# A mixer and expert layer: gates of three dense blocks added into cleared DRAM matrices instead of built by one-hot products

## The chip, the cores and the metric

The kernel runs on one core of a Trainium2 chip. Its time is the device time of one execution in microseconds. Five engines work side by side: TensorE (PE, matmuls into PSUM), VectorE (DVE), ScalarE (ACT), GpSimd (POOL) and SyncE (SP). Each executes its own list of instructions strictly in order and waits on semaphores. Transfers are issued on SP's queue, or, where an index list gives the addresses, on POOL's (indirect DMAs).

## What is computed

A layer of 1024 tokens with 1024 channels: a matrix-memory recurrence and a windowed attention side by side, merged by gates, and then an expert network (PEER). For each token, each of 8 heads picks 16 of 16384 experts by two lists of 128 sub-keys; an expert is one row of `expert_down` and one of `expert_up`.

```python
top_s, top_i = lax.top_k(s, K)                       # per head, two lists of 128 scores, K = 16
cand_s = (top_s[:, :, 0, :, None] + top_s[:, :, 1, None, :]).reshape(t, PEER_HEADS, K * K)
cand_i = (top_i[:, :, 0, :, None] * N_KEYS + top_i[:, :, 1, None, :]).reshape(t, PEER_HEADS, K * K)
best_s, best_pos = lax.top_k(cand_s, K)
idx = jnp.take_along_axis(cand_i, best_pos, axis=-1)
gate = jax.nn.softmax(best_s, axis=-1)
u = expert_down[idx]
act = jax.nn.gelu(jnp.einsum('td,thkd->thk', xb, u), approximate=False)
vv = expert_up[idx]
return jnp.einsum('thk,thkd->td', gate * act, vv)
```

## The kernel before

The tokens form 8 blocks of 128. Four groups of two blocks (0 and 1, 2 and 3, 4 and 5, 6 and 7) run one after the other through `front`: projections, attention, recurrence, gates, residual, and the expert scores. `front` streams its weights in 82 parts of 512 KB per group (`wpart`, L209, four buffers). ScalarE rounds a part to a high half and VectorE makes the low half (L215), and TensorE multiplies both (L231 to L233); some products run in plain fp32 (L229). At the end of `front` VectorE adds the residual (L614), a norm follows (L166 to L169), and TensorE computes the queries of the experts and the scores (L640). The first weight part of the next group then needs VectorE again (L215).

`topk` runs on VectorE for the blocks of the group before, at low priority, and gives each token 128 picks: row, column and gate. Then there are two ways.

- Blocks 0, 6 and 7 are sparse. `down` fetches the picked expert rows from DRAM, 128 gathers per block, each of 128 rows of 4 KB (one per token; L743, an indirect DMA on POOL), and VectorE takes the dot product of each (L756); `up` adds the weighted rows (L770). The gathers of block 0's `down` run beside the groups 1 to 3, into two buffers of a pool `gather`. Its dots are tied by order alone (no semaphore) to matmuls of the groups, the anchors: from 0.40 to 0.95 of their list (`PACE0`, `PACE1`). The gathers of `up` for block 0 and all others run in the dense stage.
- Blocks 1 to 5 are dense. All 16384 experts are computed for their 640 tokens, one column of 128 experts at a time, and multiplied by a gate matrix that is zero but for the picks. `spread` builds this matrix. For each token VectorE makes two one-hot matrices of the 128 picks (rows weighted by the gate, L727; columns, L730; a quarter of the latter on ScalarE, L732 and L733), and a 128 x 128 matmul contracts them (L735). ScalarE copies four tokens at a time into a chunk of 16 (`stage`, L736, two buffers), and SP writes the chunk to `gate_d` in DRAM (L738), 1 MB in pieces of 256 bytes. A call of four tokens comes between the matmuls of the next group's `front` (`fill`, 0.75 of one per place): block 1 in group 1, blocks 2 and 3 in group 2, blocks 4 and 5 in group 3.

The dense stage (`dense`) loads the gates of four columns at a time (L841) and multiplies them into the activations of 640 tokens (L816). In the built order a scheduler places each instruction by priority and by its own estimate of when its inputs are there; each engine then keeps that order.

Of the kernel before, what the change touches and what calls it, by code (L numbers as in the profile page):

```python
# [11 lines left out]
F32 = mybir.dt.float32  # L12
F32R = mybir.dt.float32r
I32 = mybir.dt.int32
# [5 lines left out]
NOSYNC = mybir.DependencyInfo(mybir.DependencyClass.NoSync, mybir.DependencyReason.DATA)  # L20

# [14 lines left out]
DENSE = (1, 2, 3, 4, 5)  # L36
ND = P * len(DENSE)
# [5 lines left out]
PACE0, PACE1 = 0.4, 0.95  # L43
# [11 lines left out]
def layout(inputs):  # L55
# [29 lines left out]
    a["iota"] = np.arange(P, dtype=np.float32)[None]  # L85
    return {k: np.ascontiguousarray(v) for k, v in a.items()}


def build(nc, tc, a, out, dbg=None):
# [8 lines left out]
    gp = pool("gather", 2)  # L98
# [34 lines left out]
    pos = const("pos", [P, NB], dt=I32, pool=st)  # L133
    freq = bcast("freq", 8, st)
# [59 lines left out]
    gate_d = dp.tile([P, P // GJ, ND // GT, GJ, GT], F32, name="gate_d")  # L194
# [452 lines left out]
    def topk(b):  # L647
# [15 lines left out]
        for qh in range(4):  # L663
# [23 lines left out]
            for p, n in ((0, 17), (1, 16)):  # L687
# [7 lines left out]
                else ks.tile([P, 8, 16], F32, name="dgate", bufs=2))  # L695
# [12 lines left out]
        if b in DENSE:  # L708
            r["spread"] = spread(ef, gate, DENSE.index(b))
        return r  # L710

    def spread(ef, gate, k):
# [5 lines left out]
        for c in range(P // GT):  # L718
            stage = ks.tile([P, P, GT], F32, name="stage", bufs=2)
# [20 lines left out]

    def fetch(p, table, idx, s):
        t = p.tile([P, D], F32, name="g")
        G.indirect_dma_start(out=t, out_offset=None, in_=a[table],  # L743
                             in_offset=bass.IndirectOffsetOnAxis(ap=idx[:, s:s + 1], axis=0))
        return t

    def down(r, b, pace, p):
# [14 lines left out]
        r["coef"] = coef  # L762

# [10 lines left out]
    def dense():  # L774
# [26 lines left out]
        def hidden(j, g):  # L801
# [13 lines left out]
            av_ = act.rearrange("p (c t) -> p c t", t=GT)  # L815
            V.tensor_tensor(av_, av_, g, ALU.mult)  # L816
# [22 lines left out]
        for n in range(P // EG):  # L839
            g = tp.tile([P, ND // GT, GJ, GT], F32, name="g")  # L840
            SY.dma_start(g, gate_d[:, n])  # L841
            new = []
            for e in range(EG):
                new.append(hidden(EG * n + e, g[:, :, e, :]))
# [37 lines left out]
    names = names[int(PACE0 * len(names)):int(PACE1 * len(names))]  # L882
    pace = iter([names[i * len(names) // P] for i in range(P)])
    down(res[0], 0, pace, gp)
# [22 lines left out]
```

## Time and profile before

| | us |
|---|---|
| three runs, median | 3551.62 |
| lowest, highest | 3545.43, 3563.59 |
| the profiled execution | 3545.12 |
| its span in the profile | 3543.4 |
| TensorE busy in the span | 3378.6 (95%) |
| VectorE | 2743.1 (77%) |
| ScalarE | 1363.0 (38%) |
| POOL | 985.7 (28%) |

Busy is the time in which an engine works on an instruction; transfers that it issues are not in it. The granted clock of TensorE is 0.966 of full speed over the span. The four groups end at about 370, 782, 1221 and 1714 us, told by their score matmuls (L640), and the dense stage runs from about 1746 to 3520. A row of busy times by stage shows how full an engine is, a row of waits says what an engine stood still for, and the chain that ended last names which work set the time at each moment.

### The profile page before, as it was taken

To read this page: it belongs to the slowest core of one execution; us is meant where nothing else is said; L and a number is where in the kernel's file an instruction comes from. 1 tells how busy PE (TensorE), PEld (TensorE's weight loads), DVE (VectorE), ACT (ScalarE), POOL (GpSimd) and SP (SyncE) were. 2 spreads that over 40 slices of the span, in tenths; PEclk is the share of its full clock that TensorE was granted. 3 is DMA by queue.
4 is the path that set the end of the run, shared out by engine and by line. 5 is a ranking of instruction groups with operands and counts; after the bars stand their busy time and mean duration, and the time that the engine had idled before them with its cause. 6 is when DMAs were issued, how large, how long until landed. Compare 5 with 4: busy or idle time off the path is not lost.

```text
span 3543.4 us, 55473 instructions
## 1 busy us (share of the span) xinstructions
PE 3378.6 (95%) x20579; PEld 3044.3 (86%) x20579; DVE 2743.1 (77%) x6406; ACT 1363.0 (38%) x2730; POOL 985.7 (28%) x772
## 2 busy tenths in 40 slices
PE   7999999999998789989799999999999999999999
PEld 7898988888887678887688898999989999898998
DVE  5332689739898468988598988888888888889985
ACT  6652567338574346635322222222222222222221
POOL 0000000110001221110004654545455455545542
PEclk9999999999999888999899999999999999999999
DMA  4344434874378874686727988889888888888884
GB/s 149 108 143 166 164 115 145 256 261 141 117 212 252 274 247 150 206 244 174 252 101 276 329 307 321 321 284 329 285 315 305 294 321 299 312 308 302 325 288 160
DMA packets 386670, 846.66 MB, mean 239 GB/s; under 512 B 189280, under 2 KB 195168, under 8 KB 382304
## 3 DMA queue, kind: packets, MB, share of 16 engines
q1 hardware_dynamic: 275808, 440.42, 37.7%
q0 software_dynamic: 110592, 402.70, 32.5%
q8 instruction: 162, 2.65, 0.3%
q14 instruction: 108, 0.88, 0.1%
HBM read 780.11 MB, written 62.91 MB: 238 GB/s over the span
## 4 chain that ended last, share of the span: by engine, by line
PE 66%; DVE 13%; issue 8%; DMA 7%; POOL 3%; ACT 3%; SPq 0%; POOLq 0%; DVEq 0%; ACTq 0%
PE ph L809 19%; PE pj L229 8%; PE po L830 6%; PE po L833 6%; PE po L834 6%; PE pj L231 4%; PE pj L233 4%; PE pj L232 4%; DMA g<-down,idx 3%; POOL g L743 3%; DVE oi L727 2%; PE at L735 2%; DMA w<-wmain 1%; DVE g L756 1%; DMA g<-up,idx 1%
## 5 line engine op out<-in xcount | busy, mean ns | idle before, releaser
L743 POOL DMA_INDIRECT g<-down,idx x384 | 480.2, 1250 | 1769.3 <-DVE act L756 879.2
L743 POOL DMA_INDIRECT g<-up,idx x384 | 505.3, 1316 | 732.8 <-DVE acc L770 373.9
L756 DVE CUSTOM_DVE_ANT_0 g<-g,xb 128x1024 f32<-128x1024 f32 x384 | 462.6, 1219 | 167.2 <-DMA g<-down,idx 166.6
L770 DVE SCALAR_TENSOR_TENSOR acc<-g,coef,acc 128x1024 f32<-128x1024 f32 x384 | 491.7, 1281 | 46.8 <-DMA g<-up,idx 36.8
L830 PE MATMUL po<-hu,ah 128*128 128x512 f32 x1280 | 499.2, 390 | 2.3 <-DVE y L836 2.3
L809 PE MATMUL ph<-xbh,hd 128*128 128x320 f32 x2048 | 470.6, 311 | 31.7 <-ACT hd L797 22.8
L833 PE MATMUL po<-lu,ah 128*128 128x512 f32 x1280 | 498.5, 389 | 0.0
L834 PE MATMUL po<-hu,al 128*128 128x512 f32 x1280 | 498.1, 389 | 0.0
L809 PE MATMUL ph<-xbh,ld 128*128 128x320 f32 x2048 | 470.5, 311 | 5.3 <-DVE ld L798 5.3
L809 PE MATMUL ph<-xbl,hd 128*128 128x320 f32 x2048 | 469.9, 311 | 0.0
L797 ACT CAST hu<-rawu 128x1024 fp32r<-128x1024 f32 x128 | 131.5, 1051 | 738.9 <-PE po L834 557.0
L809 PEld LDWEIGHTS ph<-xbh,hd 128*128 128x128 f32 x2048 | 346.6, 189 | 35.3 <-ACT hd L797 23.2
L215 DVE TENSOR_TENSOR wlo<-w,whi 128x1024 fp32r<-128x1024 f32 x200 | 243.3, 1218 | 142.1 <-ACT whi L214 142.0
L809 PEld LDWEIGHTS ph<-xbh,ld 128*128 128x128 f32 x2048 | 345.1, 189 | 7.0 <-DVE ld L798 6.7
L809 PEld LDWEIGHTS ph<-xbl,hd 128*128 128x128 f32 x2048 | 345.6, 189 | 0.0
L214 ACT CAST whi<-w 128x1024 fp32r<-128x1024 f32 x200 | 209.3, 1047 | 235.9 <-DMA w<-wmain 100.1
L836 DVE TENSOR_TENSOR y<-po,y 128x512 f32<-128x512 f32 x320 | 218.2, 685 | 89.0 <-PE po L834 88.5
L830 PEld LDWEIGHTS po<-hu,ah 128*128 128x128 f32 x1280 | 240.3, 188 | 53.9 <-DVE y L836 4.7
L834 PEld LDWEIGHTS po<-hu,al 128*128 128x128 f32 x1280 | 240.3, 188 | 50.5 <-DVE al L820 0.3
L833 PEld LDWEIGHTS po<-lu,ah 128*128 128x128 f32 x1280 | 240.3, 188 | 48.5
L232 PE MATMUL pj<-wlo,hT 128*128 128x256 f32 x832 | 244.9, 295 | 23.9 <-DVE wlo L215 23.9
L231 PE MATMUL pj<-whi,hT 128*128 128x256 f32 x832 | 245.9, 296 | 1.1 <-ACT whi L214 1.1
(266 smaller groups left out, 6670.2 us busy)
## 6 DMA issues: line engine op xcount, KB each, us to landing
w<-wmain SPq DMA_DIRECT2D x328, 512.0 KB
rawd<-downT SPq DMA_DIRECT2D x128, 512.0 KB
rawu<-up SPq DMA_DIRECT2D x128, 512.0 KB
gate_d<-stage SPq DMA_DIRECT2D x40, 1024.0 KB
g<-gate_d SPq DMA_DIRECT2D x32, 1280.0 KB
x<-x SPq DMA_DIRECT2D x16, 512.0 KB
sc_d<-sc SPq DMA_DIRECT2D x16, 512.0 KB
sc<-sc_d SPq DMA_DIRECT2D x32, 256.0 KB
```

The costliest lines, as they stand in the source:

```text
L215: V.tensor_tensor(lo, t, hi.bitcast(F32), ALU.subtract)
L229: ins = T.matmul(ps, lh(c), rh(c), start=first, stop=last)
L231: T.matmul(ps, lh(c), rh(c), start=first, stop=False)
L232: T.matmul(ps, lh(c), rl(c), start=False, stop=False)
L743: G.indirect_dma_start(out=t, out_offset=None, in_=a[table], in_offset=bass.IndirectOffsetOnAxis(ap=idx[:, s:s + 1], axis=0))
L756: ins = V.tensor_tensor_reduce(out=t, in0=t, in1=xb, scale=1.0, scalar=0.0, op0=ALU.mult, op1=ALU.add, accum_out=act[:, s:s + 1])
L770: ins = V.scalar_tensor_tensor(acc, t, g, acc, ALU.mult, ALU.add)
L809: ins = T.matmul(ps[:, u, 0:W], w[:, c, :], x[:, c, u * W:u * W + W], start=first, stop=last)
L830: first = T.matmul(o, ah[:, tok], uh[:, cols], start=(e == 0), stop=False)
L833: T.matmul(o, ah[:, tok], ul[:, cols], start=False, stop=False)
L834: ins = T.matmul(o, al[:, tok], uh[:, cols], start=False, stop=(e == EG - 1))
L836: V.tensor_tensor(y[:, k, cols], o, y[:, k, cols], ALU.add)
```

## The change

The gate matrices of blocks 1 to 3 no longer come from one-hot products. Three DRAM matrices `cells`, of 8 MB each, are cleared by 192 DMAs of 128 KB from a zeroed tile. `topk` computes for each pick the place in the block's matrix (`cell`), and `scatter` adds the gates there: 128 indirect DMAs per block on POOL, each of 128 values of 4 bytes (one per token) with an addition at the target. A token has no pick twice within a head, but can in two heads. So the first addition of a head waits until the 16 of the head before have landed (`SYNC`), and the other 15 follow it in order alone. The additions are tied by order to the gathers of block 0 (`BESIDE`: which gathers, for which block). `down` of block 0 starts earlier (0.32), the gather pool has three buffers, and `stage` has one. Blocks 4 and 5 keep the one-hot products. The dense stage loads the gates in two tiles and multiplies in two instructions, of 384 and 256 tokens.

```diff
-PACE0, PACE1 = 0.4, 0.95
+PACE0, PACE1 = 0.32, 0.95
+ADDED = (1, 2, 3)
+SPREAD = (4, 5)
+BESIDE = {1: (2, 44), 2: (58, 92), 3: (92, 126)}
+ZP = 64
...
-    gp = pool("gather", 2)
+    gp = pool("gather", 3)
...
+    cells = {b: dp.tile([P // EG, P, EG, P], F32, name=f"cells{b}") for b in ADDED}
+    flat = {b: t.rearrange("n i e t -> (n i e t)") for b, t in cells.items()}
+    none = st.tile([P, P * P // ZP], F32, name="none")
+    V.memset(none, 0.0)
+    clear = iter([flat[b].rearrange("(z p f) -> z p f", z=ZP, p=P)[z] for b in ADDED for z in range(ZP)])
...
     def wpart(i, q, split):
         t = wp.tile([P, 4, 256], F32, name="w", bufs=WB)
         SY.dma_start(t, a["wmain"][i, :, 4 * q:4 * q + 4, :])
+        for z in [next(clear, None)]:
+            if z is not None:
+                SY.dma_start(z, none)
...
+        if b in ADDED:
+            r["cell"] = cell = ks.tile([P, P], I32, name="cell", bufs=NA)
...
+            V.tensor_scalar(cell, pf[:, 0], float(P), tokc, ALU.mult, ALU.add)
+        if b in SPREAD:
+            r["spread"] = spread(ef, gate, SPREAD.index(b))
...
-            stage = ks.tile([P, P, GT], F32, name="stage", bufs=2)
+            stage = ks.tile([P, P, GT], F32, name="stage", bufs=1)
...
+    def scatter(b, pace):
+
+        cell, vals = res[b]["cell"], res[b]["gate"].rearrange("p h k -> p (h k)")
+        views = bass_types.dram_disjoint_views(flat[b][:, None], 16)
+        done = []
+        for h in range(8):
+            new = []
+            for s in range(16):
+                c = 16 * h + s
+                ins = G.indirect_dma_start(out=views[s], out_offset=bass.IndirectOffsetOnAxis(ap=cell[:, c:c + 1], axis=0),
+                                           in_=vals[:, c:c + 1], in_offset=None, compute_op=ALU.add)
+                if s == 0:
+                    for d in done:
+                        tc.add_manual_dep(ins.ins, d, SYNC, reason="heads")
+                else:
+                    after(ins, new[0])
+                after(ins, next(pace, None))
+                new.append(ins.ins.name)
+            done = new
...
-            V.tensor_tensor(av_, av_, g, ALU.mult)
+            V.tensor_tensor(a1_, a1_, g[0], ALU.mult)
+            V.tensor_tensor(a2_, a2_, g[1], ALU.mult)
...
+            ga = tp.tile([P, NA, EG, P], F32, name="ga")
+            gs = tp.tile([P, len(SPREAD) * P // GT, GJ, GT], F32, name="g")
+            for k, b in enumerate(ADDED):
+                SY.dma_start(ga[:, k], cells[b][n])
+            SY.dma_start(gs, gate_d[:, n])
...
+    down(res[0], 0, paced(PACE0, PACE1), gp)
+    for b, (lo, hi) in BESIDE.items():
+        scatter(b, iter([fetched[lo + i * (hi - lo) // P] for i in range(P)]))
```

The lines move: the gather is L773 in the changed kernel, the additions L804, the dots L787, the residual L631, the norm L175 to L178 and the weight split L232. In the rows below `cells_155` and `cells_156` are the matrices of blocks 1 and 2, and a count at a row's end says how often it repeats.

POOL's whole order before, apart from its set-up: block 0's gathers of `down`, then everything else.

```order
L898 MEMSET const-uint8-127 128x1
L903 UNCONDITIONAL_BRANCH
L743 DMA g<-down,idx 128x1024 x128
L743 DMA g<-up,idx 128x1024 x128
L743 DMA g<-down,idx 128x1024 x256
```

POOL now, in the last third of group 1, where block 1's additions stand between the gathers 26 to 31 (counted from 0).

```order
L804 DMA cells_155<-dgate,cell 2097152x1 x6
L773 DMA g<-down,idx 128x1024
L804 DMA cells_155<-dgate,cell 2097152x1 x10
L773 DMA g<-down,idx 128x1024
L804 DMA cells_155<-dgate,cell 2097152x1 x6
L773 DMA g<-down,idx 128x1024
L804 DMA cells_155<-dgate,cell 2097152x1 x10
L773 DMA g<-down,idx 128x1024
L804 DMA cells_155<-dgate,cell 2097152x1 x8
```

Here 40 of block 1's 128 additions moved in between gathers that stood side by side before.

POOL now, at the end of group 2, with block 2's additions between the gathers 79 to 87.

```order
L804 DMA cells_156<-dgate,cell 2097152x1 x11
L773 DMA g<-down,idx 128x1024
L804 DMA cells_156<-dgate,cell 2097152x1 x8
L773 DMA g<-down,idx 128x1024
L804 DMA cells_156<-dgate,cell 2097152x1 x6
L773 DMA g<-down,idx 128x1024
L804 DMA cells_156<-dgate,cell 2097152x1 x7
L773 DMA g<-down,idx 128x1024
L804 DMA cells_156<-dgate,cell 2097152x1 x11
L773 DMA g<-down,idx 128x1024
L804 DMA cells_156<-dgate,cell 2097152x1 x5
L773 DMA g<-down,idx 128x1024
```

The row after these is 23 additions, then one gather, and so on to the end of block 2's 128. VectorE's order at the same place before, at the residual and the norm of group 2:

```order
L614 TENSOR_TENSOR x<-pj,x 128x512
L730 TENSOR_SCALAR oj<-iota,cols 128x128
L727 TENSOR_SCALAR oi<-iota,cols 128x128
L730 TENSOR_SCALAR oj<-iota,cols 128x128
L727 TENSOR_SCALAR oi<-iota,cols 128x128
L730 TENSOR_SCALAR oj<-iota,cols 128x128
L727 TENSOR_SCALAR oi<-iota,cols 128x128 x2
L730 TENSOR_SCALAR oj<-iota,cols 128x128
L727 TENSOR_SCALAR oi<-iota,cols 128x128 x4
L756 ISA g,act<-g,xb 128x1024
L756 ISA act 128x1
```

And now (an `ISA` row with `g,act` is a dot product, the row behind it reads its sum):

```order
L631 TENSOR_TENSOR x<-pj,x 128x512
L787 ISA g,act<-g,xb 128x1024
L787 ISA act 128x1
L787 ISA g,act<-g,xb 128x1024
L787 ISA act 128x1
L631 TENSOR_TENSOR x<-pj,x 128x512 x2
L175 TENSOR_TENSOR rs_t<-rs_y 128x2
L176 SCALAR_TENSOR_TENSOR rs_t<-ms,rs_t 128x2
L177 TENSOR_SCALAR rs_t<-rs_t 128x2
L178 TENSOR_TENSOR rs<-rs_t,rs_y 128x2
L787 ISA g,act<-g,xb 128x1024
```

The one-hot compares between the residual sums are gone, and five dots (gathers 83 to 87) now stand between the norm and the first four weight splits (L232) of group 3; before, 15 dots stood there.

## Rows read from the trace of the kernel before

**Rows 1.** Busy time by stage; columns in the first row, counts in brackets.
```profile
core 0: us, PE busy (x) PEld busy (x) DVE busy (x) ACT busy (x) POOL busy (x), PEclk, DMA share, GB/s
0.00:370.00 370.00, 339.55 (x2262) 303.28 (x2262) 138.67 (x377) 184.63 (x420) 0.20 (x4) 0.96 0.42 141
370.00:782.00 412.00, 396.14 (x2681) 353.61 (x2682) 298.65 (x1093) 223.80 (x534) 28.27 (x26) 0.95 0.58 185
782.00:1221.00 439.00, 410.27 (x2726) 364.91 (x2726) 365.44 (x1352) 248.80 (x610) 46.24 (x45) 0.94 0.66 202
1221.00:1714.00 493.00, 446.78 (x2929) 392.80 (x2928) 379.36 (x1358) 252.50 (x608) 67.88 (x57) 0.92 0.67 204
1746.00:3520.00 1774.00, 1757.68 (x9863) 1605.55 (x9862) 1525.50 (x2096) 442.27 (x542) 843.09 (x640) 1.00 0.82 291
```

**Rows 2.** The same for the one-hot products (L735) alone, groups 1 and 2.
```profile
370.00:782.00 412.00, 39.76 (x256) 35.38 (x256) 0.95 0.58 185
782.00:1221.00 439.00, 79.38 (x512) 72.71 (x512) 0.94 0.66 202
```

**Rows 3.** Waits of VectorE and POOL while block 0's gathers run: total, times, longest.
```profile
DVE g L756 <- DMA g<-down,idx: 125.1, 49, 5.8
...
POOL g L743 <- DVE act L756: 610.9, 81, 144.8
```

**Rows 4.** POOL in order of time, dense stage: start, length, instruction, idle before it.
```profile
1883.14 0.94 POOL L743 DMA_INDIRECT g<-up,idx  x1 [0.30 <-issue]
1884.39 0.94 POOL L743 DMA_INDIRECT g<-up,idx  x1 [0.30 <-issue]
```

**Rows 5.** POOL in order of time, start of group 3.
```profile
1240.18 1.68 POOL L743 DMA_INDIRECT g<-down,idx  x1 [3.70 <-DVE act L756]
1242.46 1.68 POOL L743 DMA_INDIRECT g<-down,idx  x1 [0.60 <-DVE act L756]
```

**Rows 6.** The chain that ended last, block 1's products: start, length, pieces.
```profile
602.46 2.15 PE at L735 x16
```

**Rows 7.** Busy time in seven stretches of groups 1 to 3, columns as in Rows 1.
```profile
661.00:730.00 69.00, 67.47 (x368) 61.13 (x369) 34.94 (x69) 11.60 (x26) 15.57 (x15) 1.00 0.81 273
730.00:771.00 41.00, 34.84 (x164) 29.75 (x164) 9.26 (x18) 13.38 (x33) 6.38 (x6) 0.92 0.71 235
1139.00:1177.00 38.00, 32.96 (x178) 29.13 (x176) 28.00 (x87) 11.11 (x29) 8.74 (x9) 0.96 0.89 271
1177.00:1239.00 62.00, 44.45 (x215) 38.13 (x213) 26.44 (x64) 21.31 (x50) 16.06 (x16) 0.80 0.87 271
1239.00:1280.00 41.00, 28.70 (x198) 27.75 (x199) 22.18 (x32) 11.11 (x15) 12.91 (x9) 0.80 0.78 290
1367.00:1483.00 116.00, 112.52 (x716) 94.59 (x714) 98.45 (x360) 60.15 (x145) 18.78 (x16) 0.88 0.54 181
1556.00:1600.00 44.00, 40.07 (x220) 35.91 (x221) 37.54 (x126) 8.57 (x17) 8.47 (x8) 0.93 0.77 248
```

**Rows 8.** The one-hot products alone in two of these stretches.
```profile
1139.00:1177.00 38.00, 11.56 (x76) 11.04 (x76) 0.96 0.89 271
1177.00:1239.00 62.00, 6.97 (x30) 5.87 (x28) 0.80 0.87 271
```

**Rows 9.** DMA during one chunk's write: GB/s in 40 slices, and its queue.
```profile
GB/s 0 0 0 0 0 0 0 0 0 53 233 219 217 222 215 218 217 218 218 217 218 218 218 219 217 218 217 217 215 222 218 217 212 217 217 221 211 104 0 0
q1 hardware_dynamic: 4112, 1.05, 72.1%
```

**Rows 10.** Groups of instructions: line, engine, operation, count, busy us, mean ns, idle.
```profile
L735 PE MATMUL at<-oj,oi 128*128 128x128 f32 x1280 | 201.6, 290 | 23.1 <-DVE oj L730 13.1 <-DVE oi L727 5.0 <-ACT oj L733 4.8
L816 DVE TENSOR_TENSOR act<-act,g 128x640 f32<-128x640 f32 x128 | 104.7, 818 | 6.0 <-ACT act L814 6.0
L215 DVE TENSOR_TENSOR wlo<-w,whi 128x1024 fp32r<-128x1024 f32 x200 | 243.3, 1218 | 142.1 <-ACT whi L214 142.0
```

More of the change, by code (lines that the diff above doesn't have):

```diff
@@ L8 @@
 import concourse.tile as tile
+from concourse import bass_types
 from concourse import mybir
@@ L36 @@
 DENSE = (1, 2, 3, 4, 5)
+ADDED = (1, 2, 3)
+SPREAD = (4, 5)
+NA = len(ADDED)
+BESIDE = {1: (2, 44), 2: (58, 92), 3: (92, 126)}
+ZP = 64
 ND = P * len(DENSE)
@@ L133, in build @@
     pos = const("pos", [P, NB], dt=I32, pool=st)
+    tokc = const("tokc", [P, 1], pool=st)
     freq = bcast("freq", 8, st)
@@ L707, in topk @@
             probe("gate", gate, b)
-        if b in DENSE:
-            r["spread"] = spread(ef, gate, DENSE.index(b))
+        if b in ADDED:
+            r["cell"] = cell = ks.tile([P, P], I32, name="cell", bufs=NA)
+            part = kp.tile([P, 2, P], I32, name="part", tag="eq", bufs=1)
+            pf = kp.tile([P, 2, P], F32, name="partf", tag="sc")
+            V.tensor_copy(part[:, 0], ef[:, 1])
+            V.tensor_single_scalar(part[:, 1], part[:, 0], EG - 1, ALU.bitwise_and)
+            V.tensor_single_scalar(part[:, 0], part[:, 0], 2, ALU.logical_shift_right)
+            V.tensor_copy(pf, part)
+            V.scalar_tensor_tensor(pf[:, 0], pf[:, 0], float(P), ef[:, 0], ALU.mult, ALU.add)
+            V.scalar_tensor_tensor(pf[:, 0], pf[:, 0], float(EG), pf[:, 1], ALU.mult, ALU.add)
+            V.tensor_scalar(cell, pf[:, 0], float(P), tokc, ALU.mult, ALU.add)
+        if b in SPREAD:
+            r["spread"] = spread(ef, gate, SPREAD.index(b))
         return r
@@ L739, in spread @@
                 yield
+    fetched = []
     def fetch(p, table, idx, s):
         t = p.tile([P, D], F32, name="g")
-        G.indirect_dma_start(out=t, out_offset=None, in_=a[table],
-                             in_offset=bass.IndirectOffsetOnAxis(ap=idx[:, s:s + 1], axis=0))
+        ins = G.indirect_dma_start(out=t, out_offset=None, in_=a[table],
+                                   in_offset=bass.IndirectOffsetOnAxis(ap=idx[:, s:s + 1], axis=0))
+        fetched.append(ins.ins.name)
         return t
@@ L839, in dense @@
         for n in range(P // EG):
-            g = tp.tile([P, ND // GT, GJ, GT], F32, name="g")
-            SY.dma_start(g, gate_d[:, n])
+            ga = tp.tile([P, NA, EG, P], F32, name="ga")
[3 more added lines that the diff above has]
+            SY.dma_start(gs, gate_d[:, n])
             new = []
             for e in range(EG):
-                new.append(hidden(EG * n + e, g[:, :, e, :]))
+                new.append(hidden(EG * n + e, (ga[:, :, e, :], gs[:, :, e, :])))
                 if n == 0 and e == 0:
@@ L881, in build, with paced @@
     names = anchors["front"]
-    names = names[int(PACE0 * len(names)):int(PACE1 * len(names))]
-    pace = iter([names[i * len(names) // P] for i in range(P)])
-    down(res[0], 0, pace, gp)
+    def paced(lo, hi):
+        return iter([names[int((lo + i * (hi - lo) / P) * len(names))] for i in range(P)])
+    down(res[0], 0, paced(PACE0, PACE1), gp)
+    for b, (lo, hi) in BESIDE.items():
+        scatter(b, iter([fetched[lo + i * (hi - lo) // P] for i in range(P)]))
     inner.close()
```

9 lines of the change are left out of this document (6 added, 3 removed).

## The prediction

> **What bounds the kernel now.** I read the busy time by stage first [rows 1]. Four groups of two blocks run one after the other to 1714 us, and a dense stage follows. TensorE is busy 340 of 370 us in group 0, 396 of 412 in group 1, 410 of 439 in group 2, 447 of 493 in group 3, and 1758 of 1774 in the dense stage. So TensorE's instruction stream sets the end, and what can be won in the groups is the one-hot products on it and its gaps. The one-hot products (L735) have 40 us of TensorE's busy time in group 1 and 79 in group 2 [rows 2]. The gaps come mostly from the gathers of block 0. VectorE waits 125 us for gathered rows while these run, and GpSimd (POOL) waits 611 us for VectorE to free one of two buffers [rows 3]. VectorE works in order, so a late gather holds the weight splits that TensorE needs next.
>
> POOL is nearly idle: 142 us busy in 128 gathers over groups 1 to 3 [rows 1]. It is the engine that the change loads. Its prices: two gathers without a wait between them start 1.25 us apart (0.94 busy, 0.30 between) [rows 4]; at worst, beside VectorE's dots, 2.28 us (1.68 and 0.60) [rows 5]; on average 142.4/128 + 0.30 = 1.41 us.
>
> **The change part by part.**
>
> *The one-hot products of blocks 1 to 3 go.* That is 768 of 1280 matmul records [rows 10], with their VectorE, ScalarE and write work. Back to back, 16 records take 2.15 us on the chain [rows 6], so a block's 256 take 34 us. Against that, group 2 has 256 records more than group 1 and only 14 us more TensorE time [rows 1], because other matmuls run between them and share the loading of weights. I take 27 us per block, nearer to the first since VectorE's compares go too. Ends: 14 and 34. Block 1 gives 27 us, blocks 2 and 3 give 54. Of the 79 us in group 2, 18 lie in a stretch that POOL will set (below) [rows 2, 8], so 42 of the 54 count: 69 us in all.
>
> *A third gather buffer and an earlier start (0.32 of the anchors for 0.4).* TensorE's gaps in groups 1 to 3 are 16, 29 and 46 us [rows 1]. Some 50 of these 91 lie in the stretches that I cost below [rows 7]. Of the other 41, group starts explain most (group 0 has 30 without a gather), and I take 13 us as saved; ends 0 and 30.
>
> *384 indirect additions on POOL, of 128 values each.* Each writes 512 bytes, and no row shows one. The nearest row is a gather, which also turns 128 indices into addresses. Ends: 0.7 us, should half a gather's time hang on its 4 KB rows, and 2.28. I take 1.4, the mean of the gathers in the same place. Each addition takes one of eight semaphore lanes, so it also waits for the transfer eight places before it; at 1.4 us that is 11 us, longer than a gather's landing, so this is free. The first addition of each head (each 16th) waits until the 16 before it have landed, and everything on POOL stands behind it, the gathers too. VectorE's longest wait for a gather is 5.8 us [rows 3], a sign of how long 512 KB take to land; I use 5.5 for that. An addition moves far less but queues behind the same transfers, so I take 3.5 us, with ends 2 and 6.
>
> The Trainium skill's page "DMA: Bandwidth & Descriptors", section "Anatomy of one DMA — SWDGE (gpsimd) path", puts a fixed cost of about 2.0 us on each such DMA, most of it the receipt of the last write. By it the 19 waits that I count below would cost 38 us instead of 66, and the sum would be 28 us lower (an estimate from that page). No row here shows it for a DMA that adds. The same page's "Rules for kernel authors" says that transfers under 64 KB pay mostly overhead, which speaks against this change, since each addition moves half a kilobyte; by that rule rival 3 below would fall.
>
> The built order puts the additions in bunches, and the bunches decide. I count additions, gathers and heads on POOL between two places in VectorE's order, and set them against the time in which TensorE's work between those places ran before [rows 7]. Need = 1.4 x (additions + gathers) + 3.5 x heads, and 5.5 where a bunch begins, for the last gather to land. There I also allow 10 us of cover (an estimate: three gather buffers ahead, and the PSUM tiles that TensorE can still fill).
> - A1, 661 to 730 us (final part of group 1, up to its residual sums): 66 + 11, 4 heads: 127 against 79. Loss 48.
> - A2, 730 to 771 (up to the next group's first weight split): 32 + 5, 2 heads: 59 against 41. Loss 18.
> - B1, 1139 to 1177: 25 + 4, 2 heads: 53 against 48. Loss 5.
> - B2, 1177 to 1239: 55 + 5, 3 heads: 94 against 62. Loss 32. Before, 16 gathers with two buffers already stalled TensorE here (44 of 62 us busy, 7 of these one-hot products [rows 7, 8]); now the additions do.
> - B3, 1239 to 1280: 29 + 4, 2 heads: 53 against 41. Loss 12.
> - C1, 1367 to 1483: 75 + 18, 5 heads: 153 against 126. Loss 27.
> - C2, 1556 to 1600: 30 + 8, 1 head: 62 against 54. Loss 8.
>
> Sum 150 us. It is lost for good, since TensorE has no slack after these places in which to catch up.
>
> *One buffer for the one-hot chunk instead of two.* Two blocks keep 16 chunks. A chunk's write moves 1 MB at some 218 GB/s [rows 9], 5 us and its latency, and now the next chunk's first copy waits for it. The new order puts some 40 other matmuls between chunks, which hides most. I take 5 us; ends 0 and 80 (16 x 5).
>
> *192 clears of 128 KB on SyncE (SP's queue), ahead of the additions.* All of them stand between the first 43 weight loads, in group 0. At 218 GB/s [rows 9] 25 MB take 115 us of DMA time, where the engines are 42% busy over 370 us [rows 1]. So they fit on the whole, but a weight load can stand behind up to 13 of them. I take 5 us; ends 0 and 25.
>
> *The dense stage.* The gate product becomes two instructions. A product of 640 columns takes 818 ns and one of 1024 takes 1218 [rows 10], which is 1.04 ns per column and 150 ns fixed. The second instruction costs 128 x 0.15 = 19 us on VectorE, which has 249 us free there [rows 1]; I take 3. The bytes of gates loaded are the same, and POOL's last addition is well ahead of the first load.
>
> Sum: 3545 (the profiled run, 6.5 us under the median of the three) + 150 - 69 - 13 + 5 + 5 + 3 = **3626 us**, rounded to 3625, about 2% over the median.
>
> **The rivals.**
> 1. *An addition costs more than a gather*, as it reads and writes its cell. With 1.75 us and 4.5 us per head the seven stretches lose 75, 31, 16, 55, 24, 58 and 20, together 279, and the end is at 3755. For: each moves data in two directions. Against: the engine that writes addresses need not see that.
> 2. *POOL at its fastest, faster than before.* Place: the bunches A and B. VectorE stands still there, so POOL runs at the shortest period of 1.25 us, and a head costs 2 us. The stretches then lose 28, 9, 0, 18, 4, 3 and 0: 62. With the savings at their upper ends (34 + 53 + 30) and 8 of the small terms the end is at 3498. With the savings as I take them the tie is at losses of 69 us. The seven stretches hold 367 POOL instructions, so it is at a period of 1.26 us with 2 us per head, and at 1.18 with 3.5. The shortest row [rows 4] stands right on that line.
> 3. *The addition is cheap because its rows are 4 bytes*, 0.7 us. No stretch loses, B2 gains some 10, and the end is near 3420.
> 4. *No change.* Gains and stalls cancel, as at a period near 1.2 us: 3545.
>
> That the change doesn't do what it says is excluded by its order: the products of three blocks are gone, and the additions stand between the gathers.
>
> **How the numbers follow.** My forecast (3625) has 0.42; rival 1 0.20, rival 2 0.16, rival 3 0.08, rival 4 0.14. Slower by over 0.5% is the forecast and rival 1: 0.62. About 0.5% is what a measurement of this kernel can tell from no change. Same is rival 4: 0.14. Faster is rivals 2 and 3: 0.24. The range takes in rival 2 and rival 1 with a little beyond it, 3490 to 3770; rival 3 and additions at 2 us and more are left out. Slower alone spans 3570 to 3770.
>
> **What would show it.** Right: POOL's additions average 1.1 us busy or more; VectorE waits for gathers in runs of tens of us at the ends of groups 1 and 2, and TensorE's busy share falls just there. Group 1 grows, group 2 is about as long as before, group 3 longer, and the dense stage keeps its 1774 us. Wrong: additions under 0.7 us, or heads that wait under 2 us, with group 2 some 50 us shorter. It would also be wrong if the dense stage changed by more than 10 us, if ScalarE waited for the single chunk buffer, or if weight loads came late in group 0.

## The result, and the profile after

The changed kernel takes 3742.9 us (median of 3739.0 to 3746.4) against 3553.6 for the kernel before: 1.0534 times as long, interval 1.0515 to 1.0553. It is slower, as forecast, and the end lies within the range given, but it is slower by 189 us and not by 73. The end lies near that of rival 1 (3755), in which an addition costs more than a gather.

The busy time of the engines (part 1 of the page; busy us, share of the span, instructions) shows TensorE with less work than before and more idle time around it:

```profile
PE 3301.7 (88%) x19802; PEld 2968.8 (79%) x19802; DVE 2605.1 (70%) x5884; ACT 1258.6 (34%) x2442; POOL 1625.1 (43%) x1156
```

In 40 slices of the span (93.5 us each, busy share in tenths) TensorE's share falls at the ends of group 1 (slices 8 to 10) and of group 2 (13 to 16):

```profile
PE   7999998556996516988879999999999999999999
```

Busy time by stage answers to [rows 1]. The first column after the stretch is its length, then busy us and instructions of TensorE, its weight loads, VectorE, ScalarE and POOL, the granted clock, the DMA share and GB/s. The stretches are group 0, groups 1 to 3, and most of the dense stage:

```profile
0.00:374.00 374.00, 342.85 (x2287) 306.45 (x2287) 141.50 (x380) 188.46 (x426) 0.20 (x4) 0.96 0.66 210
374.00:872.00 498.00, 367.30 (x2359) 323.56 (x2360) 259.07 (x898) 181.86 (x427) 215.86 (x146) 0.84 0.52 142
872.00:1383.00 511.00, 364.36 (x2334) 320.15 (x2332) 277.43 (x933) 186.54 (x431) 258.18 (x172) 0.83 0.56 155
1383.00:1905.00 522.00, 437.77 (x2842) 390.07 (x2841) 357.95 (x1318) 248.39 (x599) 322.54 (x196) 0.88 0.69 171
1945.00:3718.00 1773.00, 1755.88 (x9831) 1599.87 (x9830) 1526.82 (x2215) 436.93 (x536) 828.34 (x640) 1.00 0.82 291
```

Group 0 and the dense stage are as before. (The border of groups 2 and 3 stands here some 20 us of work later than in [rows 1]. There it was set at 1221 us, but the last score matmuls of group 2 end at 1245.5 in the kernel before. The other three groups end, told the same way, at 374.3, 777.7 and 1713.9.) TensorE has gaps of 131, 147 and 84 us in groups 1 to 3, where [rows 1] had 16, 29 and 46. POOL has 216, 258 and 323 us of work there.

The groups of instructions (busy us and mean ns of one, then the idle time before them and what ended it) answer to [rows 10]; L804 is the addition, L763 the one-hot product, L868 and L869 the two halves of the gate product:

```profile
L804 POOL DMA_INDIRECT cells<-dgate,cell x384 | 647.3, 1686 | 157.7 <-issue 119.8 <-DMA cells<-dgate,cell 37.3 <-DMA g<-down,idx 0.6
L763 PE MATMUL at<-oj,oi 128*128 128x128 f32 x512 | 80.5, 295 | 20.8 <-DVE oj L758 10.4 <-ACT stage L764 8.7 <-ACT oj L761 1.5
L868 DVE TENSOR_TENSOR act<-act,ga 128x384 f32<-128x384 f32 x128 | 70.6, 551 | 6.0 <-ACT act L865 6.0
L869 DVE TENSOR_TENSOR act<-act,g 128x256 f32<-128x256 f32 x128 | 53.5, 418 | 0.0
```

The addition by itself (its instructions, what they wait for, and issue to landing):

```profile
L804 POOL DMA_INDIRECT cells<-dgate,cell x384: 1540/1545/7835, 617.8 to 1777.0; - x192
L804 POOLq EVENT_SEMAPHORE  x75: 17/43/12676, 616.3 to 1732.8; - x75
its engine sat idle before it (us, times) until:
  issue: 119.8, 358
  DMA cells<-dgate,cell: 37.3, 24
...
DMA to landing us min/median/max: 2.9/3.6/9.7
```

So an addition takes 1.54 us in the median and 1.69 in the mean (the 1686 ns above: 73 of the 384 take over 0.1 us longer than the median), and 0.30 us pass before it: one every 1.85 us in the median, 1.99 in the mean. Of the 24 heads 21 have a head of their block before them and wait for it. The profile puts a part of these waits under "issue", so they are counted here by place: each 16th addition has 47.0 us of idle time before it in all, 2.24 each, 1.94 more than the 0.30 that pass before any. POOL in order of time, at the end of group 1 (start, length, instruction, idle before it), shows a bunch; the gather in it is what VectorE is waiting for, and the last row is the first addition of a head:

```profile
731.24 1.56 POOL L804 DMA_INDIRECT cells<-dgate,cell  x1 [0.30 <-issue]
733.11 1.55 POOL L804 DMA_INDIRECT cells<-dgate,cell  x1 [0.30 <-issue]
734.96 1.54 POOL L804 DMA_INDIRECT cells<-dgate,cell  x1 [0.30 <-issue]
736.81 1.01 POOL L773 DMA_INDIRECT g<-down,idx  x1 [0.30 <-issue]
740.43 1.57 POOL L804 DMA_INDIRECT cells<-dgate,cell  x1 [2.61 <-issue]
```

The waits from 375 to 1900 us (who waited for whom: total, times, longest) answer to [rows 3]. The roles have changed: before, POOL stood 610.9 us for VectorE's dots, and now (from 560 to 1900 us)

```profile
POOL g L773 <- DVE act L787: 92.6, 16, 54.2
```

VectorE now waits 475 us for gathered rows, up to 47 us at once, and TensorE's long waits are for splits and sums that stand behind such a wait on VectorE (L232 is the weight split, L619 the gated sum, L308 behind L631 the norm after the residual):

```profile
DVE g L787 <- DMA g<-down,idx: 475.3, 72, 47.1
...
PE pj L249 <- DVE wlo L232: 143.1, 7, 73.3
...
PE tp L286 <- ACT scr L308: 76.8, 3, 41.9
...
PE pj L246 <- DVE gs L619: 53.2, 3, 29.9
```

### The profile page after: what moved, and what is told of

Same layout as the page of the kernel before. It is cut to its first block, busy times and chain, and to the rows that moved or that the text cites. A ratio compares the mean times of both kernels' runs of the same rounds, so it can differ in the third digit from the quotient of the medians.

```text
span 3741.6 us, 53797 instructions
## 1 busy us (share of the span) xinstructions
PE 3301.7 (88%) x19802; PEld 2968.8 (79%) x19802; DVE 2605.1 (70%) x5884; ACT 1258.6 (34%) x2442; POOL 1625.1 (43%) x1156
## 3 DMA queue, kind: packets, MB, share of 16 engines
q0 software_dynamic: 165888, 402.92, 35.0%
## 4 chain that ended last, share of the span: by engine, by line
PE 42%; DVE 8%; DMA 6%; POOL 6%; issue 4%; ACT 1%; SPq 0%; POOLq 0%; DVEq 0%; ACTq 0%
PE ph L860 18%; PE po L887 6%; PE po L883 6%; PE po L886 6%; POOL cells L804 5%; DMA g<-down,idx 2%; PE pj L246 1%; DMA g<-up,idx 1%; DMA rawu<-up 1%; POOL g L773 1%; DMA cells<-dgate,cell 1%; PE at L763 1%; DVE g L787 1%; DVE acc L821 1%; DVE ld L849 1%
## 5 line engine op out<-in xcount | busy, mean ns | idle before, releaser
L773 POOL DMA_INDIRECT g<-down,idx x384 | 482.7, 1257 | 1152.2 <-DVE sc L674 500.8
L773 POOL DMA_INDIRECT g<-up,idx x384 | 495.0, 1289 | 751.0 <-DVE acc L821 399.8
L787 DVE CUSTOM_DVE_ANT_0 g<-g,xb 128x1024 f32<-128x1024 f32 x384 | 462.8, 1220 | 502.9 <-DMA g<-down,idx 502.2
L804 POOL DMA_INDIRECT cells<-dgate,cell x384 | 647.3, 1686 | 157.7 <-issue 119.8
L821 DVE SCALAR_TENSOR_TENSOR acc<-g,coef,acc 128x1024 f32<-128x1024 f32 x384 | 491.5, 1280 | 43.9 <-DMA g<-up,idx 34.4
L232 DVE TENSOR_TENSOR wlo<-w,whi 128x1024 fp32r<-128x1024 f32 x200 | 243.2, 1219 | 128.8 <-ACT whi L231 126.5
L249 PEld LDWEIGHTS pj<-wlo,hT 128*128 128x128 f32 x832 | 167.8, 202 | 146.9 <-DVE wlo L232 144.6
```

The source lines that it names most:

```text
L249: T.matmul(ps, lh(c), rl(c), start=False, stop=False)
L773: ins = G.indirect_dma_start(out=t, out_offset=None, in_=a[table], in_offset=bass.IndirectOffsetOnAxis(ap=idx[:, s:s + 1], axis=0))
L787: ins = V.tensor_tensor_reduce(out=t, in0=t, in1=xb, scale=1.0, scalar=0.0, op0=ALU.mult, op1=ALU.add, accum_out=act[:, s:s + 1])
L804: ins = G.indirect_dma_start(out=views[s], out_offset=bass.IndirectOffsetOnAxis(ap=cell[:, c:c + 1], axis=0), in_=vals[:, c:c + 1], in_off ...
L821: ins = V.scalar_tensor_tensor(acc, t, g, acc, ALU.mult, ALU.add)
```

## Experiments

In the recorded texts A is the theory I held at that point and the other letters are its rivals; each text says what they are. Edits are against the changed kernel unless another is named.

### Without the additions

```diff
-    for b, (lo, hi) in BESIDE.items():
-        scatter(b, iter([fetched[lo + i * (hi - lo) // P] for i in range(P)]))
```

> All 384 additions are left out (the matrices of blocks 1 to 3 stay zero, so these gates are missing); the clears, the third gather buffer, the early start, the single chunk buffer and the two gate products stay. Theory A (POOL's time in bunches of additions is the loss): the groups end at 1714 - 69 - 13 + 10 = about 1640 us and the kernel takes some 3475 us, 2% under before; VectorE's wait for block 0's gathers is under 125 us. Rival B (one of the other parts costs it: the single chunk buffer, the clears, the early start): the time stays above 3600 us. What this run lies under 3545 us is the gain that the prediction put at 69 + 13 us.

Measured: 3419.4 us, 0.9611 of before (0.9594 to 0.9627). The additions cost 3743 - 3419 = 324 us, and without them the change would save 138 us (3557.9, the median before beside this run, less 3419.4), where my sum has 82 less 13 of small terms. Busy time between the same three pairs of dots (L787; from the 22nd to the 40th, the 78th to the 96th, the 100th to the last of block 0) shows where the 324 us lie. The changed kernel first, then the one without additions:

```profile
650.00:898.00 248.00, 124.16 (x668) 109.84 (x667) 45.41 (x82) 38.42 (x77) 192.33 (x126) 0.74 0.58 128
1201.00:1490.00 289.00, 144.80 (x839) 131.55 (x838) 74.88 (x184) 60.17 (x126) 235.27 (x147) 0.72 0.52 112
1527.00:1789.00 262.00, 234.04 (x1527) 205.63 (x1526) 211.18 (x774) 128.29 (x310) 203.64 (x124) 0.91 0.75 180
```

```profile
657.00:773.00 116.00, 108.41 (x634) 97.23 (x633) 45.86 (x83) 34.94 (x72) 20.56 (x18) 0.97 0.76 257
1062.00:1204.00 142.00, 133.50 (x838) 121.24 (x837) 74.72 (x184) 59.48 (x125) 20.04 (x19) 0.94 0.69 236
1233.00:1462.00 229.00, 224.68 (x1519) 198.19 (x1519) 207.77 (x773) 128.28 (x309) 34.95 (x26) 0.95 0.68 204
```

The same work takes 132, 147 and 33 us longer, 312 of the 324. In the first stretch POOL is busy 192 us, and 126 instructions with 0.30 us between add 38: 230 of 248 us, without the heads' waits. In the second it is 235 + 44 = 279 of 289. POOL sets the pace there.

### Half the additions

```diff
-        for h in range(8):
+        for h in range(4):
```

> Only heads 0 to 3 are added, 64 additions per block (the gates of heads 4 to 7 are missing). Theory A (POOL's time at 1.85 us an addition, in bunches that VectorE waits for): about half of POOL's 710 us goes, and as the ties spread 64 over fewer gathers the bunches shrink; with about half the additions in the seven stretches the losses fall from 255 to 40 to 90 us and the time to 3510 to 3570 us. Rival B (other parts): over 3650 us. Rival C (waits between heads, not POOL's own time, make the loss): the waits fall from 21 to 9, POOL's total wait on landed additions falls from 37 us to about 16, and the time by about as much, to some 3720 us.

Measured: 3552.1 us, 0.999 of before (0.9978 to 1.0002). Half of the additions cost 3552 - 3419 = 133 us, somewhat under half of 324, as theory A has it. The 9 heads that still wait for another have 17.2 us of idle time before them in all, instead of 47.0 for 21. The time fell by 191 us, so heads are not where it goes, and that rival falls.

### The other parts alone

Edit of the kernel before, with all five blocks on one-hot products; the clears are 192 writes of a zero tile, issued among the first 42 weight loads as in the changed kernel (the lines that make the matrices and the tile are left out here):

```diff
-PACE0, PACE1 = 0.4, 0.95
+PACE0, PACE1 = 0.32, 0.95
...
-    gp = pool("gather", 2)
+    gp = pool("gather", 3)
...
+        for z in [next(clear, None)]:
+            if z is not None:
+                SY.dma_start(z, none)
...
-            stage = ks.tile([P, P, GT], F32, name="stage", bufs=2)
+            stage = ks.tile([P, P, GT], F32, name="stage", bufs=1)
```

> The kernel before with all one-hot products kept, and with the changed kernel's third gather buffer, start at 0.32, single chunk buffer and 192 clears (of matrices that nothing reads). Theory A: these parts together cost little, -13 + 5 + 5 us, so about 3545 us, between 3530 and 3600; with five blocks in place of two the single chunk buffer has 40 chunks and may add up to 6 us for each that is not hidden. Rival B: one of them carries the loss, and the time is over 3650 us.

Measured: 3504.6 us, 0.9848 of before (0.983 to 0.9866), 53 us less than before: under all that I expected. My sum had 13 us of gain and 10 of loss for these parts. Two more runs took them apart.

Without the clears (edit of the kernel above):

```diff
-        for z in [next(clear, None)]:
-            if z is not None:
-                SY.dma_start(z, none)
```

> The kernel before with a third gather buffer, the start of the gathers at 0.32 and the single chunk buffer that makes the room; without the clears. Whole computation. The same with the clears took 3505 us. Theory A (the third gather buffer and the start are the gain, the clears cost nothing, since group 0 with them was as long as before): 3495 to 3510. Theory B (192 clear transfers cost some of the 5 us that the prediction gave them, or more): 3480 to 3495.

Measured: 3505.9 us, 0.9888 of before (0.9856 to 0.992). The clears cost nothing that can be told from noise: A holds.

And with the gathers' start where it was before (edit of the kernel without clears):

```diff
-PACE0, PACE1 = 0.32, 0.95
+PACE0, PACE1 = 0.4, 0.95
```

> As the run before, with the gathers' start left at 0.40 as in the kernel before: only the third gather buffer and the single chunk buffer are changed. Whole computation. Theory A (three gathers in flight instead of two is the gain): 3500 to 3520. Theory B (the earlier start is the gain): 3545 to 3560, the time before.

Measured: 3504.5 us, 0.9862 of before (0.9828 to 0.9895). The start does nothing either, and what is left is the third gather buffer with the single chunk buffer that makes its room. The two were not tried apart. VectorE's wait for gathered rows points to the gather buffer; in [rows 3] it was 125.1 us in 49 waits, and in this kernel, from 560 to 1740 us, it is:

```profile
DVE g L756 <- DMA g<-down,idx: 31.8, 17, 3.6
```

So three gathers in flight, with the single chunk buffer, are worth 42 to 53 us, and the additions in bunches spend that again.

### Plain writes instead of additions

```diff
-                                           in_=vals[:, c:c + 1], in_offset=None, compute_op=ALU.add)
+                                           in_=vals[:, c:c + 1], in_offset=None)
```

> The indirect DMAs write their values instead of adding them (no arithmetic at the target; where two heads of a token pick the same expert the later one stands, so the result differs); number, order and waits are those of the changed kernel. Theory A1 (an addition costs POOL 1.54 us and a gather 0.94 because it also reads its target): one falls to 0.94 us, the seven stretches lose about 62 to 100 us in place of 255, and the time falls to 3530 to 3590 us. Rival A2 (the price is that of any write to 128 scattered places, with or without an addition): it stays at 1.54 us and the time within 1% of 3743.

Measured: 3687.1 us, 1.0346 of before (1.0313 to 1.0379). This missed. The price per instruction went as theory A1 said, since a plain write takes POOL as long as a gather, but the time lies between the two theories' ranges:

```profile
L804 POOL DMA_INDIRECT cells<-dgate,cell x384: 952/958/7282, 622.5 to 1724.7; - x192
```

But at 384 x 0.59 us less on POOL the kernel is only 56 us faster. VectorE's wait for gathers is 112 us instead of 475. In its place TensorE stands idle before L246 with no cause in the profile ("issue"), for 97 us where the changed kernel has at most 0.2. From 375 to 1900 us:

```profile
PE pj L246 <- issue: 97.0, 36, 20.6
```

So either the write into DRAM has a price of its own, or something else holds the engines.

### Reads instead of additions

```diff
+        junk = gp.tile([P, P // 2], F32, name="junk", bufs=1)
...
-                ins = G.indirect_dma_start(out=views[s], out_offset=bass.IndirectOffsetOnAxis(ap=cell[:, c:c + 1], axis=0),
-                                           in_=vals[:, c:c + 1], in_offset=None, compute_op=ALU.add)
+                ins = G.indirect_dma_start(out=junk[:, c % (P // 2):c % (P // 2) + 1], out_offset=None, in_=flat[b][:, None],
+                                           in_offset=bass.IndirectOffsetOnAxis(ap=cell[:, c:c + 1], axis=0))
```

> Left out: the gates of blocks 1 to 3 are never added; each addition is replaced by an indirect read of the same 128 cells into a small tile, in the same place of GpSimd's order, so nothing is written to DRAM there. The plain writes of the experiment before took GpSimd 0.96 us each, like a gather, and yet the time stayed at 3687 us. Theory A (GpSimd's instructions are what costs, at their own price; the rest of the plain writes' loss lay in the writing): a read costs 0.95 + 0.3 us, and a sum over the 128 dots of the kernel without additions, with GpSimd in series, gives 130 to 155 us on its 3419: 3550 to 3575. Theory B (any 384 small indirect transfers among the gathers hold the other engines, whichever way they go): as with the plain writes, 3660 to 3710. Theory C (the write into DRAM and its landing is all of the price): 3420 to 3470.

Measured: 3710.1 us, 1.0446 of before (1.0402 to 1.0489): the upper end of B, so the write into DRAM is not it. The trace shows what happens instead. POOL in order of time at the end of group 1, where reads and gathers follow each other every 1.25 us until 733 us:

```profile
730.88 0.94 POOL L804 DMA_INDIRECT junk<-cells,cell  x1 [0.30 <-issue]
732.13 0.94 POOL L804 DMA_INDIRECT junk<-cells,cell  x1 [0.30 <-issue]
733.38 0.95 POOL L804 DMA_INDIRECT junk<-cells,cell  x1 [0.30 <-issue]
744.59 0.94 POOL L773 DMA_INDIRECT g<-down,idx  x1 [10.26 <-DVE hTlow L294]
```

TensorE, ScalarE and VectorE in the same time:

```profile
708.00 0.58 PE L246 MATMUL pj<-w,mixT 128*128 128x256 f32 x1 [0.84 <-issue]
728.87 3.78 PE L246 MATMUL pj<-w,mixT 128*128 128x256 f32 x8 [20.29 <-issue]
```

```profile
740.98 0.63 ACT L292 ACTIVATE hT<-tp,gains 128x128 fp32r<-128x128 f32 x2 [72.47 <-remote]
```

```profile
728.39 0.42 DVE L619 TENSOR_TENSOR gs<-pj,gs 128x256 f32<-128x256 f32 x1 [34.20 <-issue]
...
740.99 0.42 DVE L619 TENSOR_TENSOR gs<-pj,gs 128x256 f32<-128x256 f32 x1 [11.71 <-remote]
...
743.09 1.22 DVE L787 CUSTOM_DVE_ANT_0 g<-g,xb 128x1024 f32<-128x1024 f32 x1
```

ScalarE copies at 741 us what TensorE's transposes had finished at 698, and the dot at 743 takes a gather that was issued at 698. TensorE itself stops within a run of matmuls for 20.29 us; a few get through at 729, and everything goes on at 741, some 7 us after POOL's last read. In the changed kernel no dot of the first two stretches comes more than 16 us after its gather's issue; here it is up to 71. So what I priced as POOL's time alone has a second effect at this rate, and the plain writes show the same (up to 68 us between a gather's issue and its dot).

### Reads with a pause

```diff
+        pad = gp.tile([P, 32], F32, name="pad", bufs=1)
...
+                after(ins, rest[0])
+                for _ in range(2):
+                    m = G.memset(pad, 0.0)
+                    after(m, rest[0] if _ else ins.ins.name)
+                    rest[0] = m.ins.name
```

(against the kernel with reads; in the second run `range(5)`)

> The kernel with 384 indirect reads in place of the additions (3710 us; the gates of blocks 1 to 3 are left out), with two small fills of a 128x32 tile on GpSimd behind each read, so that a read comes every 1.5 to 1.6 us and not every 1.25. In the trace of the reads alone TensorE, ScalarE, VectorE and SyncE stood still together while GpSimd issued back to back (697 to 741 us), and went on when it paused. Theory A (issuing back to back at 1.25 us holds up the other engines' semaphores): with the pauses the holding ends, and GpSimd's serial sum at 1.5 us gives 3419 + 200 to 240 = 3620 to 3660: slower instructions, faster kernel; the idle time of TensorE before line 246 without a cause in the profile falls from 207 us to near 0. Theory B (it has to do with small reads and plain writes as such, not with their rate): 3710 to 3800, and the idle time without a cause stays.

Measured: 3665.6 us, 1.0312 of before (1.0275 to 1.0349): 6 us over A's range and 44 us faster than without the fills, though POOL has more to do. The reads now come every 1.42 us, and TensorE's idle time before the matmuls of L246 without a cause is 2.0 us, where the reads alone have 95.6 (the 207 in the text on record counts their weight loads too):

```profile
705.63 0.95 POOL L806 DMA_INDIRECT junk<-cells,cell  x1
706.58 0.32 POOL L816 MEMSET pad<- 128x32 f32 x2
707.05 0.95 POOL L806 DMA_INDIRECT junk<-cells,cell  x1
```

```profile
PE pj L246 <- issue: 95.6, 45, 20.3
```

```profile
PE pj L246 <- issue: 2.0, 4, 0.7
```

(From 560 to 1900 us, the reads alone and then the reads with two fills.) VectorE's wait for gathers is back at 308 us: the dots wait for POOL again and not for what holds everything.

> As the run before with five fills behind each read, so that a read comes every 1.8 to 2.1 us, as often as an addition or more seldom. The gates of blocks 1 to 3 are left out. Theory A (only GpSimd's serial time counts once nothing else is held up): like the additions in the same places at 1.85 us, 3743, or up to 3850 at 2.1 us; no idle time without a cause. Theory B (the memory side of an addition is part of its price): under 3700 at the same spacing.

Measured: 3724.9 us, 1.0491 of before (1.0457 to 1.0525), a read every 1.97 us, and no such idle time over 0.2 us. It lies between the two theories' numbers, 18 us under A's, and A stands better: reads that touch no DRAM cell for writing cost 306 us over the kernel without additions when they come nearly as often as additions, and additions cost 324. VectorE waits 454 us for gathers, where it waits 475 beside the additions. So most of what an addition costs here is POOL's time. Not all of it is shown to be: on a line through the two runs with fills (3666 at 1.42 us, 3725 at 1.97), reads every 1.85 us would take some 3712 us, an estimate that leaves 31 us of the additions' price open.

### The additions spread out

```diff
-BESIDE = {1: (2, 44), 2: (58, 92), 3: (92, 126)}
+BESIDE = {1: (0.38, 0.62), 2: (0.64, 0.80), 3: (0.80, 0.98)}
...
-        scatter(b, iter([fetched[lo + i * (hi - lo) // P] for i in range(P)]))
+        scatter(b, paced(lo, hi))
```

This ties them to points of TensorE's work instead of to gathers. The sum behind theory A takes the 128 dots of the kernel without additions at their times, lets POOL do its instructions in series at the measured prices (1.84 an addition, 1.26 a gather, 1.55 a head, three buffers, 3 to 5 us to land), and adds up what each dot comes late. For the changed kernel it gives 277 to 292 us, where 324 were measured.

> Whole computation: the changed kernel with only the places of the additions changed. All three blocks are added, tied to points spread over 0.38 to 0.98 of TensorE's work: two or three behind most gathers, four or five at the end, bunches of up to 31. Theory A: 3419 + 128 to 145 by the serial sum = 3547 to 3564, some 180 us under the changed kernel and about the time before. Theory B: as the changed kernel, 3743.

Measured: 3593.4 us, 1.0109 of before (1.0088 to 1.0131): 149 us less than the changed kernel, with the same 384 additions at the same price (1538/1552 ns shortest and median). It is 29 us over A's range, as the changed kernel is over the sum. The sum's prices are medians, and the mean addition is longer (1686 ns there, 1739 here). Done again with the mean prices of each run, the sum gives 344 to 356 us for the changed kernel and 197 to 212 here, more than the 324 and 174 measured, so the measured losses lie between the two sums.

Two blocks added, the other three on one-hot products (besides the `scatter` line above; against the changed kernel):

```diff
-ADDED = (1, 2, 3)
-SPREAD = (4, 5)
+ADDED = (1, 2)
+SPREAD = (3, 4, 5)
...
-BESIDE = {1: (2, 44), 2: (58, 92), 3: (92, 126)}
+BESIDE = {1: (0.40, 0.67), 2: (0.69, 0.96)}
```

> Whole computation. Blocks 1 and 2 are added, block 3 goes back to one-hot products, and the additions are tied to points spread over TensorE's work from 0.40 to 0.96 of it: two or three stand behind most gathers, with bunches of 22, 26 and 11. Theory A (an addition costs only where GpSimd falls behind the dots): base 3505 - 2 x 28 (a third of 3505 - 3419 per block) = 3448; the same serial sum gives 22 to 37 us of loss: 3470 to 3490. Theory B (each addition costs the same wherever it stands, 324 us / 384 = 0.84 us): 3448 + 216 = 3664.

Measured: 3468.7 us, 0.975 of before (0.972 to 0.9779), 1 us under A's range; B is 195 us off.

One block added:

```diff
-ADDED = (1, 2, 3)
-SPREAD = (4, 5)
+ADDED = (1,)
+SPREAD = (2, 3, 4, 5)
...
-BESIDE = {1: (2, 44), 2: (58, 92), 3: (92, 126)}
+BESIDE = {1: (0.42, 0.95)}
```

> Whole computation. Only block 1 is added, blocks 2 to 5 keep one-hot products; its additions are spread from 0.42 to 0.95 of TensorE's work, about one behind each gather, with bunches of 16, 11 and 11. Theory A (cost only where GpSimd falls behind): 3505 - 28 = 3476, plus 1 to 16 us: 3477 to 3492, faster than the kernel before and than the other parts alone. Theory B (0.84 us for each addition): 3476 + 108 = 3584.

Measured: 3477.8 us, 0.9788 of before (0.9766 to 0.981), as A says; B is 106 us off.

Two blocks spread out beat the kernel before by 2.5% and the other parts alone by 36 us. VectorE's wait for gathers there is 115.8 us in 37 waits. A third block costs 125 us more than it saves. With it POOL has little to spare: in the 1085 us (571 to 1656) in which block 0's dots run, it is busy 765.6 us with 481 instructions, and 0.30 us between them add 144, without the heads' waits.

## Why the prediction was right, and where it was wrong

*The mechanism.* Right: POOL becomes the engine that sets the pace where the order puts additions in bunches, the late gather holds VectorE, and VectorE holds TensorE's weight splits. The rows I named for this are there: additions over 1.1 us, waits of VectorE of up to 47 us, TensorE's share falling at the ends of groups 1 and 2, a dense stage of the same length.

*The price of an addition* is the step that failed. I took 1.4 us per POOL instruction, the mean of the gathers [rows 1], for want of a row with an addition. It is 1.54 + 0.30 = 1.85 us in the median, and 1.99 in the mean, which is what my 1.4 was. Both lie within the ends of 0.7 and 2.28, but I chose by the nearest row, and a gather isn't the same thing: a plain write costs what a gather costs (0.96 us), and the adding is the other 0.59.

*The wait of a head* was too dear: 3.5 us taken, 1.94 measured. (Under 2 us was one of my signs of being wrong; group 2, which was to be shorter with it, was not.) By the Trainium skill's 2.0 us ("DMA: Bandwidth & Descriptors", "Anatomy of one DMA — SWDGE (gpsimd) path") I would have been nearer; the landing itself takes longer than that figure (2.9 us at least, 3.6 in the median), but much of it is over when the next head comes up.

With the median price and 1.94 per head (gathers left at 1.41) my seven stretches lose 72, 29, 13, 53, 22, 53 and 20 us: 263 instead of 150. With the mean price they lose 306. The sum is then 3545 + 263 - 69 - 13 + 13 = 3739 or, with 306, 3782; the result, 3743, lies between. So the price, less what the heads give back, is large enough for the 117 us by which I was low. A run at nearly my price bears this out in part: reads every 1.42 us take 3666 us, 77 under the changed kernel and 40 over the forecast.

*The places* were only half right, and the end hides it. The 7200 matmuls named `pj` come in nearly the same order in both kernels (199 differ), so the same places can be timed in both. A1 loses 54 us there, A2 with the first matmuls of group 2 behind it 68, B1 6, B2 56, B3 7, C1 7 and C2 20: 218 in all. Another 33 us go from 1280 to 1367 us of the kernel before, which I didn't count. So A2 and B2 lose far more than I gave them, and C1 less (27 forecast, 53 with the right price). That the sum with the right price comes near the result is luck in this respect. Why C1 loses so little stays open.

*The savings* come out near what the sum used, 82 less 13: between the stretches the changed kernel gains 29, 20 and 15 us (595 to 662, 778 to 1139 and 1483 to 1557 us of the kernel before). Taken without additions they are 138 us, 53 of them from the third gather buffer and the chunk buffer (I had 13) and 85 from the products (69). The rest of the 138 presumably lies in the places where POOL sets the pace; that wasn't tried by itself. One reading behind the 27 us per block was wrong. Since [rows 1] ends group 2 some 24 us early, the 14 us more of TensorE's time there are 39 by the last score matmuls (388.3 and 427.3 us busy), and 14 was no lower end. The 27 stood up all the same: from the run without clears to the one without additions, group 1 falls by 27 us for one block and group 2 by 67 for two.

*Clears, dense stage, chunk buffer.* The clears: 5 us taken, none measured; group 0 ends at 374.0 us (374.3 before), at a DMA share of 0.66 instead of 0.42 [rows 1]. The dense stage: as said; the two gate products take 551 + 418 ns for 818 before [rows 10], 19 us on VectorE, under cover. The single chunk buffer: ScalarE waits 10.5 us for it in all and TensorE 8.7 behind that; 5 were taken. That ScalarE waited for it at all was one of my signs of being wrong, but it is no part of the 117 us.

*By group.* I said that group 2 would be about as long as before. Told by the last score matmuls (777.7 and 1245.5 us before, 872.9 and 1383.8 after) it takes 511 us instead of 468. B2 loses 56 us where I gave it 32, and the stretch before it gains only 20.

*Rivals.* Rival 1 was near with the price (1.75 us) and with 4.5 us per head had the end (3755), at a chance of 0.20; its heads were more than twice too dear, so that it ends 12 us from the result is in part luck. Its reason against, that the engine that writes addresses need not see the adding, is refuted: POOL's own instruction is longer. Rivals 2 to 4 needed a price of 1.25 us or less. A plain write comes near it (0.96 + 0.30); even then the runs with plain writes and reads (3687 and 3710 us) show that no gain would have come, for a reason none of them knew.

## What to carry to other kernels

Price an instruction on the engine that issues it from a row of the same instruction, and where there is none, from a small run of its own before its place is planned; here an indirect addition costs POOL 1.85 us (1.99 in the mean) and a gather 1.25 to 1.41. Compare means with means. Then look at bunches, not at totals: the same 384 additions cost 324 us tied to the gathers and 174 spread over TensorE's work (3593 - 3419), and 256 of them spread out cost some 20 (3469 against 3505 - 2 x 28 = 3448, an estimate that shares the 3505 - 3419 evenly among three blocks). Take a change apart before it is judged: a third gather buffer with its single chunk buffer was worth 1.4%, and the part that gave the change its name spent it.

## What the runs showed of the hardware

- An indirect addition of 128 values takes POOL 1.54 us, an indirect plain write of the same values 0.96 and a read 0.94 (medians); between two of them pass 0.30 us. In packets of POOL's queue, an addition makes 144 (165888 against 110592 without, over 384) and a plain write 32 (122880). That the longer instruction writes out more of them fits this, but wasn't tried by itself. The Trainium skill says ("Perfetto Trace Analysis", "DMA Instruction — SWDGE (GPSIMD)") that such an instruction's span in the profile ends when the descriptors are written, not when the data is moved; the traces agree, as an addition of 1.54 us lands 3.6 us after its issue.

```profile
q0 software_dynamic: 165888, 402.92, 35.0%
```

```profile
q0 software_dynamic: 122880, 402.92, 31.4%
```

(The changed kernel, then the one with reads, which has as many packets as plain writes: packets, MB, share of time.)

- Small indirect reads and plain writes issued back to back every 1.25 us, 30 instructions on end in the place shown, hold up the other engines: a result waits 43 us for ScalarE, TensorE stops for 20 us within a run of matmuls, and all goes on when POOL pauses. With 0.32 us of other work behind each read the idle time without a cause falls from 95.6 to 2.0 us, and the kernel is 44 us faster. The additions, at 1.85 us, don't show it. Which part of the chip is held up, the profile doesn't say; that stays open.
- Where POOL sets the pace, TensorE's granted clock falls too, to 0.72 and 0.74 against 0.94 and 0.97 for the same work without additions, and its 3034 matmuls in the three stretches take 503 us instead of 467 for 2991. These are means of two levels: from 764 to 800 us, with TensorE idle throughout, the clock stands at 0.50 (1.2 GHz), and from 812 to 836, with TensorE busy throughout, at 1.00 (2.4 GHz).
